# Two weight units of a query projection in Strassen's seven products, and another timetable for early weight sums

## The chip, the cores and the metric

One core of a Trainium2 chip runs the kernel once; the other cores have no part in it. The metric is the device time of that execution in microseconds. TensorE (PE) does the matrix products into eight PSUM banks, VectorE (DVE), ScalarE (ACT) and GpSimd (POOL) work on tiles in SBUF, and DMA queues fed by SyncE (SP) and POOL bring the weights from HBM.

## The reference, cut to what matters

One decoder layer for 256 tokens of width 2048, in float32: a projection for two kinds of attention, the attentions, an output projection, a gated feed-forward block of width 5632, and a gated embedding branch, with RMS norms between.

```python
a = rmsnorm(h, attn_norm)
proj = a @ w_in            # q of 8 latent heads | latent c_kv | shared rope key | q, k, v of 8 block heads
kv = rmsnorm(c_kv) @ w_ukv # keys and values of the latent heads
h += concat(mla_attention(...), moba_attention(...)) @ w_o
f = rmsnorm(h)
h += (silu(f @ w_gate) * (f @ w_up)) @ w_down
g = sigmoid(rmsnorm(h) @ w_ple_gate)
h += g * (p @ w_ple_proj)
return rmsnorm(h)
```

The weights hold nearly all of the data and of the work: each of their 128x512 blocks meets two tiles of 128 tokens.

## The kernel before, in words

**Products.** Both sides of a product are split into a high part in TensorE's rounded float32 type and a low part, the rest. `three` (L392 to L399) makes each product of three matmuls: high by high, low by high (activation's low part, L398), high by low (weight's low part, L399). The weight's high part is a ScalarE copy (`split_hi`, L352), its low part a VectorE subtraction (`split_lo`, L363).

**Units and groups.** A group is one projection of up to 1024 columns; `group` cuts it into units of two 128-row tiles of the weight, mostly a 256x1024 piece of 1 MB. In order the groups are: ga (latent, rope key, part of v), q0 (first 1024 query columns), u0 (keys and values of the first four latent heads; called the key group here, to keep it apart from the up group u0), q1, u1, qk0, qk1, v, wo0, wo1, then gate and up groups g0, u0, g1, d1, u1, and so on to gu5, with pieces of the down projection (d) between, dl, and the last groups. Each plain unit is 24 matmuls of 512 columns (2 row tiles, 2 halves of columns, 2 token tiles, 3 matmuls).

**Strassen units.** In the gate and up groups, and in two units of dl1, a unit's 2x2 block product is made in seven block products instead of eight: 21 matmuls. They come in four turns (`seven`, L439 on), wait for sums of activation blocks (four of them, made by `act_transpose` or `sums_of`) and of weight blocks (L362, L365, L366, made by VectorE in place in the raw buffer after the load). Behind a group's last Strassen unit the products meet in a tile U (L464 to L468), and the group's last unit is added to it (L427).

**Early sums.** For twelve Strassen units of g1 to u4 (the last of a gate group, the last two of an up group) the weight sums are made long before. `early_sums` is a generator, begun at q0's first unit: it loads the unit's 1 MB through POOL's queue into the tile "more_sums" (L375), waits until TensorE has been given 38,400 more columns, does three VectorE operations (L381 to L383), stores the result to HBM (L385) and goes on to the next. The late load of such a unit then brings sums instead of weights, into two raw buffers (L224 to L226).

**Order.** Everything is issued by one loop over units and turns (from L1294); each engine works through its own instructions in that order. In each turn the loop first collects the splits that may be made (`jobs`), issues their high parts, runs `step()`, which moves every waiting task on by one piece (rotations, transposes, attention heads, early sums; L500 on), issues the low parts and then the turn's products. When a split may be issued is set by `plan` (L243 on): high and low parts lie in a ring of 12 places of 512 columns, a job takes places in turn without wrapping, and it may be issued only in a turn behind the one that last used any of them. Plain units take 4 places. From g0 on the ring is longer. The raw buffers are three, from g0 on five.

```python
jb.first = at
jb.wait = max(last.get(x, -1) for x in range(at, at + places))
...
while nxt < len(jobs) and jobs[nxt].unit in raw and jobs[nxt].wait < j and jobs[nxt].unit <= i + (3 if i > 1 else 1) and \
        (jobs[nxt].unit <= i + 2 or i >= wide and units[jobs[nxt].unit].asked < i) and \
        not (u.sevens_end and 0 <= n < 3 and jobs[nxt].unit > i + 1):
    todo.append(jobs[nxt])
```

Behind q0, `after_q_mla` rotates q (L568 to L573, twelve VectorE operations) in the first step of the key group and transposes it in the next (L711).

Of the kernel before, what the change touches and what calls it, by code (L numbers as in the profile page):

```python
# [35 lines left out]
def kernel(ctx, tc, x, p, positions, attn_norm, w_in, kv_norm, w_ukv, w_o, ffn_norm,  # L36
# [152 lines left out]
    def group(name, srcs, ks, chunks, lhs, evac, pool=None, singles=0, per=2, sums=None, sevens=(), adding=(),  # L189
              order=None, swap=False, bank0=0, deep=False, into=None, early=()):  # L190

        pairs = [ks[i:i + 1] for i in range(singles)] + [ks[i:i + per] for i in range(singles, len(ks), per)]
        st = {"banks": None, "begun": set()}
        for i, pr in enumerate(pairs):
            u = Unit()
            u.name, u.srcs, u.ks, u.chunks, u.lhs, u.st = name, srcs, pr, chunks, lhs, st
            u.first, u.last, u.evac, u.pool = i == 0, i == len(pairs) - 1, evac, pool
            u.order = order or [(c, t) for c in range(len(chunks)) for t in range(NT)]
            u.idx, u.store, u.again, u.into = i, None, None, into
# [168 lines left out]
    def early_sums():  # L368

        for u in units:  # L370
            if not u.early:
                continue
            f = big.tile([128, 4, 512], F32, name="wsums", tag="more_sums")
# [4 lines left out]
            while columns[0] < since + 38400:  # L378
                yield 1
# [61 lines left out]
    def seven(u, turn):  # L441
# [18 lines left out]
        if turn == 3 and u.sevens_end:  # L460
            U = S["U"] = big.tile([128, NT, 1024], F32, name="U", tag="vb")
# [14 lines left out]
    def sums_of(parts, k0, pairs, at, tag="vb"):  # L476

        for n, kk in enumerate(pairs):
# [6 lines left out]
            hi, lo = (aT[i][:, at + 2 * n:at + 2 * n + 2] for i in range(2))  # L485
# [5 lines left out]
            split_psum(hi, lo, some)  # L491
            yield 1

    def sum_at(pairs, at):
        def f(k, j):
            o = at + 2 * pairs.index(k) + j // 2
            return tuple(aT[i][:, o, j % 2 * 128:j % 2 * 128 + 128] for i in range(2))
        return f

# [243 lines left out]
    def after_kv(half):  # L743
        def g():
# [4 lines left out]
            yield 1  # L749
            for i in range(4):  # L750
# [74 lines left out]
    oM_alloc()  # L825
# [37 lines left out]
    group("q0", [(wi, 0, 1024)], K16, C2, a_l, q0_evac)  # L863
# [175 lines left out]

    def mixed(name, order=((0, 0), (1, 0), (0, 1), (1, 1))):  # L1040
# [7 lines left out]
                    early=sevens[-2 if name[0] == "u" else -1:] if name[-1] in "1234" else (), order=list(order) if sevens else None,  # L1048
# [40 lines left out]
    LAST_SUMS = (36, 38)  # L1089
    for hc in range(2):  # L1090
        pairs = LAST[hc].split()
        group(f"dl{hc}", [(wd, hc * 1024, hc * 1024 + 1024)], [2 * int(x.strip("S")) + i for x in pairs for i in range(2)],
              C2, ff_l, add_evac(hc * 1024, ssp, norm_half(8 * hc, G_PLE, ssp if hc else None, "rp", 1 if hc else 6)),
              sevens=tuple(i for i, x in enumerate(pairs) if x[0] == "S"), sums=sum_at(LAST_SUMS, 8),
              order=[(0, 0), (1, 0), (0, 1), (1, 1)] if hc else None, deep=True, into=hc * 1024, swap=not hc)
# [198 lines left out]
    for i, u in enumerate(units):  # L1294
        asking[0] = i
        if i < wide:
            load(i + 3)
        if u.name == "q0" and u.idx == 0:
            add(early_sums())
# [8 lines left out]
        if u.name == "dl0" and u.idx == 0:  # L1308
            add(sums_of(ffT[4], 32, LAST_SUMS, 8), 5)
# [6 lines left out]
        for n in range(max(1, len(u.turns))):  # L1316
# [16 lines left out]
            if n % 2 == 0:  # L1333
# [48 lines left out]
```

## Time and profile before

| | |
|---|---|
| median of 3 runs | 1189.46 us (1189.06 to 1189.85) |
| the profiled execution | 1189.34 us |
| its span | 1187.6 us |
| PE, DVE, ACT, POOL busy | 99%, 79%, 60%, 5% |
| splits on DVE, L363, into the ring | 301, 436.5 us |
| splits on ACT, L352, into the ring | 303, 370.4 us |
| HBM read, written | 250.41 MB, 25.17 MB |

The span is the time between the first and the last instruction on the chip. A row of a timeline gives start and duration in us, engine, line, operation, the tile written and those read, with shapes, and in brackets how long the engine had been idle before it and what released it. The table of waits gives the total in us, how often and the longest. A matmul's row lasts longer than it holds TensorE, since matmuls are pipelined; the distance between starts tells the pace.

### The profile page before, as it was taken

The numbers are of one execution on the slowest core, as the hardware profiler recorded it, in microseconds if no ns is written. First come the engines' busy times: TensorE is split into PE (matmuls) and PEld (weight loads), VectorE is DVE, ScalarE is ACT, GpSimd is POOL, SyncE is SP. The second block draws the span as 40 slices with busy tenths as digits, with TensorE's granted clock in tenths as the row PEclk, the third lists the DMA queues.
The fourth block names the chain that finished last, engine by engine and source line by source line (L and its number), as shares of the span: only waits on it lengthen the run. The fifth ranks groups of instructions, "written<-read, shape, count | busy, mean of one in ns | idle before, by whom it ended". The sixth has DMA issues, their size and how long they took to land.

```text
span 1187.6 us, 14600 instructions
## 1 busy us (share of the span) xinstructions
PE 1175.0 (99%) x5486; PEld 982.7 (83%) x5486; DVE 938.5 (79%) x1109; ACT 708.4 (60%) x904; POOL 54.6 (5%) x76
## 2 busy tenths in 40 slices
PE   9999999999999999999999999999999999999996
PEld 7888888899888888888888888888888888888886
DVE  6656656766666678998999898989998999897474
ACT  6735745456555754566657575767575756465453
POOL 5200000000000000000000000000000000000000
PEclk9999999999999999999999999999999999999999
DMA  9775876667784776396978797778878795836631
GB/s 309 244 264 180 293 267 230 227 216 270 258 321 165 283 247 240 107 333 165 336 206 296 214 330 223 261 222 321 237 262 243 266 270 207 339 139 219 209 107 71
DMA packets 86647, 284.92 MB, mean 240 GB/s; under 512 B 5612, under 2 KB 10016, under 8 KB 82224
## 3 DMA queue, kind: packets, MB, share of 16 engines
q1 hardware_dynamic: 77664, 239.36, 56.9%
q0 software_dynamic: 8624, 44.10, 13.7%
q8 instruction: 43, 0.70, 0.2%
q10 hardware_dynamic: 288, 0.52, 0.1%
q14 instruction: 28, 0.23, 0.1%
HBM read 250.41 MB, written 25.17 MB: 232 GB/s over the span
## 4 chain that ended last, share of the span: by engine, by line
PE 90%; DVE 6%; ACT 2%; issue 1%; DMA 1%; ACTq 0%; POOL 0%; DVEq 0%; POOLq 0%
PE bank L399 29%; PE bank L397 28%; PE bank L398 28%; DVE ringl L363 2%; PE bank L138 1%; ACT ringh L352 1%; PE bank L1028 1%; DMA raw<-in_w_o 1%; DVE most L363 1%; PE bank L590 0%; DVE morel L363 0%; PE bank L619 0%; PE bank L593 0%; PE bank L711 0%; ACT att L603 0%
## 5 line engine op out<-in xcount | busy, mean ns | idle before, releaser
L352 ACT CAST ringh<-raw 128x1024 fp32r<-128x1024 f32 (+4 forms) x303 | 370.4, 1258 | 272.2 <-PE bank L398 123.6
L363 DVE TENSOR_TENSOR ringl<-raw,ringh 128x1024 fp32r<-128x1024 f32 (+4 forms) x301 | 436.5, 1473 | 108.2 <-ACT ringh L352 103.7
L397 PE MATMUL bank<-ringh,aT 128*128 128x512 f32 (+3 forms) x721 | 278.5, 386 | 0.0
L399 PE MATMUL bank<-ringl,aT 128*128 128x512 f32 (+3 forms) x721 | 273.6, 380 | 0.1
L398 PE MATMUL bank<-ringh,aT 128*128 128x512 f32 (+3 forms) x721 | 273.4, 379 | 0.0
L399 PEld LDWEIGHTS bank<-ringl,aT 128*128 128x128 f32 x721 | 135.5, 188 | 25.5 <-DVE ringl L363 0.7
L397 PEld LDWEIGHTS bank<-ringh,aT 128*128 128x128 f32 x721 | 135.8, 188 | 23.9 <-ACT aT L124 0.3
L398 PEld LDWEIGHTS bank<-ringh,aT 128*128 128x128 f32 x721 | 135.7, 188 | 23.7
L363 DVE TENSOR_TENSOR morel<-raw,moreh 128x1024 fp32r<-128x1024 f32 (+2 forms) x68 | 87.4, 1305 | 5.1 <-ACT moreh L352 4.5
L352 ACT CAST moreh<-raw 128x1024 fp32r<-128x1024 f32 (+2 forms) x70 | 77.6, 1143 | 21.1 <-DVE raw L362 11.4
L397 PE MATMUL bank<-ringh,ffTh 128*128 128x512 f32 x212 | 82.6, 389 | 0.0
L398 PE MATMUL bank<-ringh,ffTl 128*128 128x512 f32 x212 | 82.5, 389 | 0.0
L399 PE MATMUL bank<-ringl,ffTh 128*128 128x512 f32 x212 | 82.5, 389 | 0.0
L352 ACT CAST most<-raw 128x1024 fp32r<-128x1024 f32 (+2 forms) x58 | 57.7, 1021 | 37.2 <-DVE raw L362 16.4
L363 DVE TENSOR_TENSOR most<-raw,most 128x1024 fp32r<-128x1024 f32 (+2 forms) x58 | 67.6, 1182 | 1.3 <-ACT most L352 1.0
L362 DVE TENSOR_TENSOR raw<-raw 128x1024 f32<-128x1024 f32 x50 | 61.2, 1225 | 1.7
L398 PEld LDWEIGHTS bank<-ringh,ffTl 128*128 128x128 f32 x212 | 39.8, 188 | 8.3
L399 PEld LDWEIGHTS bank<-ringl,ffTh 128*128 128x128 f32 x212 | 39.8, 188 | 8.2
L397 PEld LDWEIGHTS bank<-ringh,ffTh 128*128 128x128 f32 x212 | 39.8, 188 | 8.2
L397 PE MATMUL bank<-moreh,aT 128*128 128x512 f32 x92 | 36.0, 391 | 0.0
L366 DVE TENSOR_TENSOR raw<-raw 128x512 f32<-128x512 f32 x50 | 34.6, 692 | 1.7
L399 PE MATMUL bank<-morel,aT 128*128 128x512 f32 x92 | 35.8, 389 | 0.0
(361 smaller groups left out, 1929.5 us busy)
## 6 DMA issues: line engine op xcount, KB each, us to landing
raw<-in_w_down SPq DMA_DIRECT2D x44, 1024.0 KB, 7.2
raw<-in_w_gate SPq DMA_DIRECT2D x36, 1024.0 KB, 7.2
raw<-in_w_up SPq DMA_DIRECT2D x32, 1024.0 KB, 7.8
raw<-in_w_in SPq DMA_DIRECT2D x40, 512.0 KB, 4.8
raw<-in_w_o SPq DMA_DIRECT2D x16, 1024.0 KB, 7.2
raw<-in_w_ple_gate SPq DMA_DIRECT2D x16, 1024.0 KB, 5.1
raw<-in_w_in SPq DMA_DIRECT2D x8, 1024.0 KB, 4.9
wsums<-in_w_up POOLq DMA_DIRECT2D x8, 1024.0 KB, 7.8
```

Of the source, the lines that this page charges most:

```text
L138: nc.tensor.transpose(b[:, (2 * i + t) * 128:(2 * i + t + 1) * 128], part[:, t, i * 128:(i + 1) * 128], ident)
L352: nc.scalar.copy(h[:, :, c0:c1], r[:, :, c0:c1])
L362: tt(f[:, 0:2], f[:, 1:2].to_broadcast([128, 2, 512]), f[:, 0:4:3], op=ALU.subtract)
L363: tt(l[:, :, c0:c1], r[:, :, c0:c1], h[:, :, c0:c1].bitcast(F32), op=ALU.subtract)
L366: tt(f[:, 2], f[:, 2], f[:, 3], op=ALU.subtract)
L397: nc.tensor.matmul(b, xh, h, start=start, stop=False)
L398: nc.tensor.matmul(b, xl, h, start=False, stop=False)
L399: nc.tensor.matmul(b, xh, l, start=False, stop=stop)
L1028: nc.tensor.transpose(b[:, (2 * i + t) * 128:(2 * i + t + 1) * 128], st[:, t, (k + i) * 128:(k + i + 1) * 128], ident)
```

## The change

Units 5 and 6 of q0 (counted from 0) become Strassen units. Their activation sums are made by `sums_of` from aT in the steps of q0's units 3 and 4 into a tile of their own on the tag "f2h"; U lies on the tag "f0h", and the tile oM, which had these tags from the start, is now made when the first heads begin. q0's plain units now come as two jobs of 2 places each; a Strassen unit takes 2, 1, 2 and 2. In q0's Strassen units `step()` runs only in the first turn, and only if there are free banks.

The early sums begin sooner and in two tiles: one generator from ga's unit 5 for two units in the tile "f0l", another from ga's unit 8 for the others in "more_sums"; both take from one list. The wait is 34,816 columns instead of 38,400, and no sum is made while "crowded" holds: q0 from unit 3 on, v from unit 1 on, wo0 before unit 4. Which units have early sums changes too: g1 has two instead of one, u4 one instead of two; there are twelve as before.

```diff
-    def early_sums():
-
-        for u in units:
-            if not u.early:
-                continue
-            f = big.tile([128, 4, 512], F32, name="wsums", tag="more_sums")
+    todo_early = []
+
+    def early_sums(tag, enough=99):
+
+        made = 0
+        while todo_early and made < enough:
+            u = todo_early.pop(0)
+            made += 1
+            f = big.tile([128, 4, 512], F32, name="wsums", tag=tag)
...
-            while columns[0] < since + 38400:
+            while columns[0] < since + 34816 or S["crowded"]:
                 yield 1
...
-            U = S["U"] = big.tile([128, NT, 1024], F32, name="U", tag="vb")
+            U = S["U"] = big.tile([128, NT, 1024], F32, name="U", tag=u.home)
...
+    def sums_tile(pairs):
+        def f(k):
+            if "four" not in S:
+                S["four"] = big.tile([128, 2, 2, 4, 128], F32R, name="four", tag="f2h")
+            return tuple(S["four"][:, i, pairs.index(k)] for i in range(2))
+        return f
...
+            if half == 0:
+                oM_alloc()
...
-    group("q0", [(wi, 0, 1024)], K16, C2, a_l, q0_evac)
+    SA = sums_tile((10, 12))
+    group("q0", [(wi, 0, 1024)], chunks=C2, lhs=a_l, evac=q0_evac, sums=sum_at(SA), home="f0h",
+          **by_pairs("0 1 2 3 4 S5 S6 7"))
...
+    EARLY = dict(g1=2, u1=2, g2=1, u2=2, g3=1, u3=2, g4=1, u4=1)
...
-                    early=sevens[-2 if name[0] == "u" else -1:] if name[-1] in "1234" else (), order=list(order) if sevens else None,
+                    early=sevens[-EARLY.get(name, 0):] if name in EARLY else (), order=list(order) if sevens else None,
...
+        S["crowded"] = (u.name == "q0" and u.idx > 2 or u.name == "v" and u.idx > 0 or
+                        u.name == "wo0" and u.idx < 4)
+        if u.name == "ga" and u.idx == 5:
+            todo_early.extend(x for x in units if x.early)
+            add(early_sums("f0l", 2))
+        if u.name == "ga" and u.idx == 8:
+            add(early_sums("more_sums"))
         if u.name == "q0" and u.idx == 0:
-            add(early_sums())
+            add(sums_of(aT, 0, (10, 12), SA, "xh"), 3)
...
-            if n % 2 == 0:
+            if n % 2 == 0 and (i >= wide or not u.strassen or n == 0 and B["rot"]):
                 step()
```

The rest of the change gives `sums_of` a function for where its results go, and writes the two dl groups through the new helper `by_pairs`, with the same units and places as before.

More of the change, by code (lines that the diff above doesn't have):

```diff
@@ L189, in group @@
     def group(name, srcs, ks, chunks, lhs, evac, pool=None, singles=0, per=2, sums=None, sevens=(), adding=(),
-              order=None, swap=False, bank0=0, deep=False, into=None, early=()):
+              order=None, swap=False, bank0=0, deep=False, into=None, home="vb", early=()):
         pairs = [ks[i:i + 1] for i in range(singles)] + [ks[i:i + per] for i in range(singles, len(ks), per)]
@@ L198, in group @@
             u.order = order or [(c, t) for c in range(len(chunks)) for t in range(NT)]
-            u.idx, u.store, u.again, u.into = i, None, None, into
+            u.idx, u.store, u.again, u.into, u.home = i, None, None, into, home
             u.strassen, u.sevens_first, u.sevens_end = i in sevens, i in sevens[:1], i in sevens[-1:]
@@ L474, in seven, with sums_of @@
                 add(join())
-    def sums_of(parts, k0, pairs, at, tag="vb"):
-        for n, kk in enumerate(pairs):
+    def sums_of(parts, k0, pairs, dst, tag="vb"):
+        for kk in pairs:
             both = big.tile([128, 2, 2, SEQ], F32, name="both", tag=tag)
@@ L490, in sums_of, with spare_sums, f, sum_at @@
             tt(four[:, 3], a12, four[:, 1], op=ALU.subtract)
-            split_psum(hi, lo, some)
+            split_psum(*dst(kk), four)
             yield 1
[L494 to L497, printed above, removed]
-        return f
+    def spare_sums(pairs, at):
+        def f(k):
+            o = at + 2 * pairs.index(k)
+            return tuple(aT[i][:, o:o + 2].rearrange("q a (b c) -> q (a b) c", b=2) for i in range(2))
+        return f
+    def sums_tile(pairs):
+        def f(k):
+            if "four" not in S:
+                S["four"] = big.tile([128, 2, 2, 4, 128], F32R, name="four", tag="f2h")
+            return tuple(S["four"][:, i, pairs.index(k)] for i in range(2))
+        return f
+    def sum_at(dst):
+        return lambda k, j: tuple(x[:, j] for x in dst(k))
+    def by_pairs(text):
+        pairs = text.split()
+        sevens = tuple(i for i, x in enumerate(pairs) if x[0] == "S")
+        ks = [2 * int(x.strip("S+")) + i for x in pairs for i in range(2)]
+        adding = tuple(i for i, x in enumerate(pairs) if x[-1] == "+")
+        return dict(ks=ks, sevens=sevens, adding=adding, order=[(0, 0), (1, 0), (0, 1), (1, 1)] if sevens else None)
     tasks, posts = [], []
@@ L1088 @@
     LAST = ('16 17 18 19 20 21', '16 S18 S19 17 20 21')
-    LAST_SUMS = (36, 38)
+    SL = spare_sums((36, 38), 8)
     for hc in range(2):
[L1091 to L1095, printed above, removed]
+        group(f"dl{hc}", [(wd, hc * 1024, hc * 1024 + 1024)], chunks=C2, lhs=ff_l,
+              evac=add_evac(hc * 1024, ssp, norm_half(8 * hc, G_PLE, ssp if hc else None, "rp", 1 if hc else 6)),
+              sums=sum_at(SL), deep=True, into=hc * 1024, swap=not hc, **by_pairs(LAST[hc]))
     def p_l(k, t):
@@ L1308 @@
         if u.name == "dl0" and u.idx == 0:
-            add(sums_of(ffT[4], 32, LAST_SUMS, 8), 5)
+            add(sums_of(ffT[4], 32, (36, 38), SL), 5)
         if u.name == "dl0" and u.idx == 2:
```

2 lines of the change are left out of this document (removed).

## The prediction

> **What bounds the kernel now.** I read the page first, then TensorE's waits, then timelines of TensorE and VectorE around each place that the change touches.
>
> ```profile
> span 1187.6 us, 14600 instructions
> PE 1175.0 (99%) x5486; PEld 982.7 (83%) x5486; DVE 938.5 (79%) x1109; ACT 708.4 (60%) x904; POOL 54.6 (5%) x76
> ...
> DVE  6656656766666678998999898989998999897474
> ...
> PE bank L399 <- DVE most L363: 0.9, 1, 0.9
> PE bank L619 <- DVE att L596: 0.3, 1, 0.3
> PE bank L613 <- ACT att L609: 0.3, 1, 0.3
> ```
>
> TensorE is busy for 1175.0 of 1187.6 us, and once it has started its waits are three short ones. So the time is the number of columns that TensorE streams, plus the few places where VectorE's low halves (L363) come late. VectorE has room in the first third (6 tenths) and hardly any from the gate and up groups on (9 tenths). Work taken off TensorE counts in full; work put on VectorE counts only where the split that TensorE wants next stands behind it. The profiled execution took 1189.34 us, 1.74 over its span and 0.12 under the median of 1189.46. All sums below are made against 1189.34.
>
> **Part 1: two Strassen units in q0.** A plain unit is 24 products of 512 columns, a Strassen unit 21. The first unit of the group behind q0 gives the pace and the point at which the second one wants its low half:
>
> ```profile
> 97.16 0.39 PE L397 MATMUL bank<-ringh,ckvT 128*128 128x512 f32 x1
> ...
> 102.61 0.60 PE L711 MATMUL bank<-ident,stage 128*128 128x128 f32 x4
> 102.97 0.48 PE L397 MATMUL bank<-ringh,ckvT 128*128 128x512 f32 x1
> ...
> 103.52 0.40 PE L399 MATMUL bank<-ringl,ckvT 128*128 128x512 f32 x1
> ```
>
> Twenty-four products take 102.61 - 97.16 = 5.45 us, 0.227 each. Six fewer save **1.36 us**, all on the bound engine. The Trainium skill ("TensorE: Matmul & The Clock Gate", section "Wait — 56ns, not 53.3ns?") states N / 2.4 GHz plus about 2.5 ns, which is 216 ns for 512 columns and would make this 1.29 us; the trace's 0.227 is longer, and the measurement decides.
>
> What it adds lies on VectorE. Its row before, and the same operations where the kernel already has them (late groups):
>
> ```profile
> 62.40 2.28 DVE L363 TENSOR_TENSOR ringl<-raw,ringh 128x2048 fp32r<-128x2048 f32 x1
> ...
> 93.64 2.29 DVE L363 TENSOR_TENSOR ringl<-raw,ringh 128x2048 fp32r<-128x2048 f32 x1 [3.15 <-ACT ringh L352]
> 95.85 1.22 DVE L381 TENSOR_TENSOR wsums<-wsums 128x1024 f32<-128x1024 f32 x1
> ...
> 98.44 0.28 DVE L568 TENSOR_TENSOR ra<-stage,tabs 128x128 f32<-128x128 f32 x1
> ...
> 101.55 2.35 DVE L363 TENSOR_TENSOR ringl<-raw,ringh 128x1024 fp32r<-128x1024 f32 x2
> ...
> 912.17 1.22 DVE L362 TENSOR_TENSOR raw<-raw 128x1024 f32<-128x1024 f32 x1
> ...
> 918.92 1.22 DVE L362 TENSOR_TENSOR raw<-raw 128x1024 f32<-128x1024 f32 x1
> ...
> 1015.99 1.28 DVE L427 TENSOR_TENSOR U<-U,bank 128x512 f32<-128x512 f32 x2
> ...
> 1038.42 0.68 DVE L483 TENSOR_TENSOR both<-ffTh,ffTl 128x512 f32<-128x512 f32 x1
> ...
> 1041.46 0.68 DVE L122 TENSOR_TENSOR ffT<-bank,ffT 128x512 fp32r<-128x512 f32 x1
> ...
> 1059.64 0.69 DVE L465 TENSOR_TENSOR U<-U,bank 128x512 f32<-128x512 f32 x1 [0.30 <-PE bank L399]
> ...
> 1062.29 2.35 DVE L363 TENSOR_TENSOR ringl<-raw,ringh 128x1024 fp32r<-128x1024 f32 x2
> ```
>
> A plain split costs 2.2 us (93.64 to 95.85). A Strassen unit without early sums costs 6.75 (912.17 to 918.92), one pair's activation sums 3.04 (1038.42 to 1041.46), forming U 2.65 (1059.64 to 1062.29), an add to U 0.64, an early weight sum 2.59 (95.85 to 98.44), the rotation of q 3.1 (98.44 to 101.55). VectorE is free at 64.7 (62.40 + 2.28), at the third unit's step. From there to the end of q0 it gets one early weight sum (2.6), the plain splits of unit 4, of unit 7 and of the next group's first unit (6.6), two pairs of sums (6.1), two Strassen units (13.5), U (2.65) and four adds (2.55): 34.0 us, ending at 98.7. TensorE ends q0 at 97.16 - 1.36 = 95.80. VectorE, which was a whole unit ahead, is now 2.9 us behind. Inside the group this is just hidden: sixth and seventh unit get their low halves with some tenths to spare.
>
> **Part 2: what stands next in VectorE's queue.** Two things meet at the first unit of the key group (u0 in the code, behind q0).
>
> The first is the ring. It has 12 places. In the old plan each unit has 4, and the key group's second unit takes those of q0's unit 6, so its split is queued in q0's last turn (the row at 93.64). With the change the five plain units end at place 3, the sixth unit gets 4 to 10, the seventh 0 to 6 (its first pair of places doesn't fit at 11), the eighth 7 to 10, the key group's first unit 0 to 3, its second 4 to 7. Place 7 belongs to the eighth unit, so this split can be queued only in the key group's first turn, behind that turn's step.
>
> The second is the step. The tile "f0l" is loaded at ga's unit 5; at ga's unit 8 there are 3 x 11,520 = 34,560 columns, 256 short of 34,816, so its sum runs at q0's unit 0 and its second is due 36,864 columns later, at unit 3, where "crowded" holds it. The tile "more_sums" is loaded at ga's unit 8, summed at q0's unit 2 (36,096 columns), and its next is held as well. At the key group's first unit "crowded" is off, and **both** run, ahead of the rotation of q and of the split.
>
> So VectorE, in order, does 98.7 + 5.2 + 3.1 + 2.2 = 109.2, and with the hand-over TensorE goes on at about 109.2. It wants that low half 103.52 - 97.16 = 6.36 us after q0's end, at 102.16. **Stall: 7.0 us.** If VectorE had no arrears at all, the last add still waits for the last bank: a hand-over (0.30 in the row at 1059.64) and 0.64 after q0's end, so 95.8 + 0.95 + 10.5 = 107.25, a stall of 5.1. With half a microsecond of hand-overs to ScalarE inside the Strassen units it is 7.6. I take 7.0, since the list of work is complete. Nothing behind it gives it back: TensorE is the bound before and after.
>
> Moving the loads of the first sums into ga and the tile "oM" behind the keys I cost at nothing: the first load leaves when POOL has done the rotary angles, as today's does, and U's and the sums' readers end long before head_mla writes "oM". The skipped steps in the two Strassen units cost nothing either; the tasks that could run then are the held sums.
>
> **Part 3: which units have early sums.** g1 gets a second one (its unit 5), u4 loses one (also its unit 5).
>
> ```profile
> 502.99 0.39 PE L398 MATMUL bank<-most,sumsmore_sums 128*128 128x512 f32 x1
> 504.28 0.50 PE L399 MATMUL bank<-most,sumsmore_sums 128*128 128x512 f32 x1 [0.90 <-DVE most L363]
> ...
> 925.66 1.23 DVE L362 TENSOR_TENSOR raw<-raw 128x1024 f32<-128x1024 f32 x1
> ...
> 928.73 1.22 DVE L363 TENSOR_TENSOR most<-raw,most 128x1024 fp32r<-128x1024 f32 x1
> ...
> 930.68 0.39 PE L399 MATMUL bank<-most,sumsmore_sums 128*128 128x512 f32 x1
> ```
>
> The stall at 504.28 is g1's unit 5: 1.29 instead of 0.227, 1.06, with a tenth after it: **1.2 us**, and 2.6 us less on VectorE just ahead of it takes it away. In u4 the third product pair of unit 4 is split at 928.73 + 1.22 = 929.95 and wanted at 930.68, a lead of 0.73. A unit without early sums takes 6.74 on VectorE (918.92 to 925.66) against 21 x 0.227 = 4.77, and loses 1.97. Unit 5 today has early sums and loses nothing; without them its third turn comes 1.97 - 0.73 = 1.24 late, with the tenth **+1.3 us** (0 to 1.5). The stall moves from g1 to u4.
>
> **Part 4: nothing behind the keys.** Three units' columns are now enough for a sum, so the other eight follow at every third unit's worth of columns, the last at v's unit 0; today they run on through v (273.35 below) into wo0.
>
> ```profile
> 266.96 1.48 DVE ringl L363
> ...
> 270.69 0.31 PE L399 MATMUL bank<-ringl,aT 128*128 128x320 f32 x1
> ...
> 271.80 1.48 DVE ringl L363
> 273.35 1.14 DVE wsums L381
> ...
> 275.41 0.31 PE L399 MATMUL bank<-ringl,aT 128*128 128x320 f32 x1
> ...
> 277.36 7.75 DMA raw<-in_w_o
> ...
> 289.27 0.38 PE L620 MATMUL bank<-pTb,vb 128*128 128x128 f32 x2
> 289.96 0.70 PE L619 MATMUL bank<-pTb,vb 128*128 128x256 f32 x2 [0.30 <-DVE att L596]
> ...
> 303.96 0.82 PE L613 MATMUL bank<-ident,att 128*128 128x128 f32 x6
> 305.08 0.84 PE L613 MATMUL bank<-ident,att 128*128 128x128 f32 x3 [0.29 <-ACT att L609]
> 305.84 0.70 PE L619 MATMUL bank<-pTb,vb 128*128 128x256 f32 x2
> ...
> raw<-in_w_o SPq DMA_DIRECT2D x16, 1024.0 KB, 7.2
> ```
>
> In v VectorE loses ground to TensorE; its leads at units 4 and 5 are 270.69 - 268.44 = 2.25 and 275.41 - 273.28 = 2.13. Today's sum (273.35) comes after them; one of 2.6 at unit 0 comes before them: **+0.5** (0 to 0.6). The chain then goes through the load of w_o, which leaves when a raw buffer comes free at 277.36, at the same point either way. It took 7.75 us, the median of its kind is 7.2, and the sums' loads and stores are gone. Behind it TensorE stalls twice: small products take 0.09 each (four from 102.61 to 102.97), but two from 289.27 take 0.69 and nine from 303.96 take 1.88, some 0.5 and 1.1 too long. I take half: **-0.8** (0 to -1.6). The Trainium skill ("Trainium Kernel Development and Optimization", "Key Constraints") says that transfers of all queues interleave on the same 16 DMA engines, by which the POOL queue's traffic does slow this load; how much no row here separates.
>
> **Sum.** -1.36 + 7.0 - 1.2 + 1.3 + 0.5 - 0.8 = +5.4: 1194.8, and with 0.12 for the median **1194.9 us**. With all ends together: -1.36 + 5.1 - 1.2 - 1.6 = +0.9 (1190.3) to -1.36 + 7.6 - 1.2 + 1.5 + 0.6 = +7.1 (1196.6).
>
> **Rivals.**
>
> The split gets ahead (the other side). If the second key unit's split is queued in q0's last turn as today, the weight sums stand behind it and hide under the key group. It decides at one place of the ring: if the eighth unit didn't hold place 7. For it speaks today's order (93.64 ahead of 95.85); against it the places as counted. The 7.0 goes: -1.6, **1187.9 us**, no change that can be told; with u4 free and both w_o stalls gone -4.2, 1185.3, faster. 0.17.
>
> More is late than I count. If VectorE's arrears reach q0's own seventh unit, or its raw buffers come free so late that the keys' loads land late, about 1.5 us come on top: **1196.5** and over. For it: some tenths of slack only. Against: a late group has two such units in a row without a stall, if with a longer ring. 0.07.
>
> The saving isn't had. If the seventh unit waits as long as six products last, the 1.36 is given back within the group; but the same lateness then shortens the later stall, as VectorE's chain is the longer one: 1194.9 again, from other places. 0.04.
>
> **Chances.** The forecast has 0.72. A measurement of this kernel tells 0.2% (2.4 us) from no change. Faster, under 1187.1: a part of the first rival, 0.08. Within 1187.1 to 1191.8: the rest of it, 0.09, and the forecast's low end, 0.08: 0.17. Slower: 0.75. The forecast's own range is 1190.3 to 1196.6; to hold 8 in 10 I take it from 1187.3 to 1197.2, with most of the first rival in it.
>
> **What would show it.** TensorE's waits should show one of 5 to 7.6 us, on L399 of the key group's second unit, ended by VectorE's L363, and VectorE's timeline before it two early sums in a row, twelve rotations, then a 128x2048 split. q0 should be 1.36 us shorter. The 504 wait should be gone and one of about 1.3 us stand one unit (4.8 us) behind the place that is 930.68 today. If the key group's second unit starts its third product without a wait, the forecast is wrong, and the result lies near 1188.

## The result and the profile after

The changed kernel takes 1199.18 us, median of six runs (1197.99 to 1199.93), against 1189.32 of the kernel before in six runs (1189.06 to 1189.85). The ratio is 1.0081, with an interval of 1.0068 to 1.0094: 0.8% slower, by more than the forecast, and above the upper end of its range. The profiled execution took 1197.99 us with a span of 1196.1, 8.5 over the span of before, and is the fastest of the six. Medians are of undisturbed executions: two single ones of later kernels, 1992.82 us with the hold in the keys and 1326.83 us with the filled wait, came at mean granted clocks of 0.56 and 0.84 and are left out.

The page of the kernel after (busy times, then the slices of VectorE and of TensorE's granted clock, the share of full speed that the chip allows it):

```profile
span 1196.1 us, 14660 instructions
PE 1176.1 (98%) x5480; PEld 981.9 (82%) x5480; DVE 957.0 (80%) x1147; ACT 713.1 (60%) x919; POOL 54.4 (5%) x76
...
DVE  5797766857456687998989898989998999897474
...
PEclk9998999999999999999999999999999999999999
```

There are six matmuls fewer (5480 against 5486), and yet PE is busy for 1.1 us more. The slices show why: the fourth, which is 90 to 120 us, has a clock of 8 tenths, and before has 9 or more in all forty. The waits of TensorE (total, how often, longest):

```profile
PE bank L402 <- DVE ringl L363: 8.1, 3, 6.7
...
PE bank L138 <- ACT stage L970: 0.4, 1, 0.4
```

The longest is the one forecast. TensorE's timeline at the key group's second unit (start, duration, line, operation):

```profile
101.88 0.48 PE L400 MATMUL bank<-ringh,ckvT 128*128 128x512 f32 x1
102.20 0.40 PE L401 MATMUL bank<-ringh,ckvT 128*128 128x512 f32 x1
109.28 0.80 PE L402 MATMUL bank<-ringl,ckvT 128*128 128x512 f32 x1 [6.68 <-DVE ringl L363]
109.87 0.63 PE L400 MATMUL bank<-ringh,ckvT 128*128 128x512 f32 x1
110.30 0.63 PE L401 MATMUL bank<-ringh,ckvT 128*128 128x512 f32 x1
...
112.43 0.50 PE L400 MATMUL bank<-ringh,ckvT 128*128 128x512 f32 x1
112.77 0.39 PE L401 MATMUL bank<-ringh,ckvT 128*128 128x512 f32 x1
```

From 102.20 to 109.28 there are 7.08 us where 0.227 belong: the wait costs 6.85. But look at the starts behind it. They stand 0.43 us apart, not 0.227, up to 112.43. Eight steps from 109.28 to 112.77 take 3.49 us where 1.82 belong: another **1.67 us**. The table by stretches (PE, PEld, DVE, ACT, POOL busy, then granted clock, DMA share, GB/s) names the reason:

```profile
104.00:109.00 5.00, 0.00 (x0) 0.00 (x0) 4.76 (x13) 0.08 (x1) 0.80 (x2) 0.68 0.77 315
109.00:113.00 4.00, 3.72 (x10) 2.96 (x10) 2.50 (x3) 0.69 (x1) 0.46 (x1) 0.54 0.70 208
105.82:112.65 6.83, 3.37 (x8) 2.69 (x9) 5.61 (x8) 0.69 (x1) 0.71 (x1) 0.50 0.66 227
```

The clock granted to TensorE falls while it waits and is 0.54 in the stretch in which it starts again. The last row gives the bounds of the half speed: it begins at 105.82, some 3.2 us after the last product ahead of the wait, and ends at 112.65, 3.4 us after TensorE goes on. VectorE's timeline over the wait:

```profile
96.26 2.47 DVE L430 TENSOR_TENSOR U<-U,bank 128x512 f32<-128x512 f32 x4
98.65 1.22 DVE L384 TENSOR_TENSOR wsums<-wsums 128x1024 f32<-128x1024 f32 x1
...
101.24 1.22 DVE L384 TENSOR_TENSOR wsums<-wsums 128x1024 f32<-128x1024 f32 x1
...
106.73 0.29 DVE L592 TENSOR_TENSOR qpT<-qpT,ra 128x128 f32<-128x128 f32 x1
106.94 4.56 DVE L363 TENSOR_TENSOR ringl<-raw,ringh 128x2048 fp32r<-128x2048 f32 x3
```

The four adds end at 98.7, two early sums stand behind them, then the rotation, then the split: the order and the end that Part 2 gave. Three smaller places on TensorE, and what ScalarE does ahead of the second:

```profile
88.00 0.50 PE L402 MATMUL bank<-ringl,four 128*128 128x512 f32 x1
...
400.27 0.95 PE L138 MATMUL bank<-ident,stage 128*128 128x128 f32 x4 [0.45 <-ACT stage L970]
...
943.88 0.50 PE L402 MATMUL bank<-ringl,sumsmore_sums 128*128 128x512 f32 x1 [1.15 <-DVE ringl L363]
```

```profile
396.12 3.70 ACT L352 CAST ringh<-raw 128x2048 fp32r<-128x2048 f32 x2
399.72 1.70 ACT L970 ACTIVATE stage<-h,rs 128x256 f32<-128x256 f32 x4
```

At 400.27, ahead of g0, TensorE waits for a scale on ScalarE that stands behind two casts; the kernel before has no wait there. The account of the spans, in us:

| term | forecast | in the trace |
|---|---|---|
| six products fewer | -1.36 | -1.36 |
| q0's sixth to eighth unit late (0.41 at 88.00, 0.13 at 91.3) | 0 | +0.54 |
| wait in the key group | +7.0 | +6.85 |
| half clock behind it | not thought of | +1.67 |
| g1's unit 5 | -1.2 | -1.17 |
| u4's unit 5 | +1.3 | +1.42 |
| v | +0.5 | +0.40 |
| behind v, heads ahead of wo0 | -0.8 | -0.56 |
| g0's first step | not thought of | +0.89 |

This adds to +8.7. The profiled run was 0.4 earlier at q0's start, which the change doesn't touch; that leaves 8.3 of the 8.5. The median is 1.2 us above the profiled run, where the kernel before has its profiled run at the median; the fourth experiment bears on this.

### The profile page after: what moved, and what is told of

It is laid out like the page before. It is cut to its first block, busy times and chain, and to the rows that moved or that the text cites. A ratio compares the mean times of both kernels' runs of the same rounds, so it can differ in the third digit from the quotient of the medians.

```text
span 1196.1 us, 14660 instructions
## 1 busy us (share of the span) xinstructions
PE 1176.1 (98%) x5480; PEld 981.9 (82%) x5480; DVE 957.0 (80%) x1147; ACT 713.1 (60%) x919; POOL 54.4 (5%) x76
## 4 chain that ended last, share of the span: by engine, by line
PE 89%; DVE 6%; ACT 2%; issue 1%; DMA 1%; SPq 0%; DVEq 0%; ACTq 0%
PE bank L402 28%; PE bank L400 28%; PE bank L401 28%; DVE ringl L363 2%; PE bank L138 1%; ACT ringh L352 1%; PE bank L1050 1%; DMA raw<-in_w_o 1%; PE bank L609 0%; PE bank L730 0%; PE bank L638 0%; PE bank L612 0%; ACT att L622 0%; DVE wsums L384 0%; PE bank L632 0%
## 5 line engine op out<-in xcount | busy, mean ns | idle before, releaser
L352 ACT CAST ringh<-raw 128x1024 fp32r<-128x1024 f32 (+4 forms) x315 | 374.8, 1226 | 266.2 <-PE bank L401 116.7
L363 DVE TENSOR_TENSOR ringl<-raw,ringh 128x1024 fp32r<-128x1024 f32 (+4 forms) x313 | 441.1, 1433 | 94.6 <-ACT ringh L352 90.1
L400 PE MATMUL bank<-ringh,aT 128*128 128x512 f32 (+3 forms) x711 | 274.5, 386 | 0.0
L402 PE MATMUL bank<-ringl,aT 128*128 128x512 f32 (+3 forms) x711 | 270.0, 380 | 0.3 <-DVE ringl L363 0.2
L401 PE MATMUL bank<-ringh,aT 128*128 128x512 f32 (+3 forms) x711 | 269.3, 379 | 0.0
L400 PEld LDWEIGHTS bank<-ringh,aT 128*128 128x128 f32 x711 | 133.8, 188 | 23.4 <-ACT aT L124 0.3
L401 PEld LDWEIGHTS bank<-ringh,aT 128*128 128x128 f32 x711 | 133.7, 188 | 23.3
L363 DVE TENSOR_TENSOR morel<-raw,moreh 128x1024 fp32r<-128x1024 f32 (+2 forms) x68 | 87.5, 1306 | 10.3 <-ACT moreh L352 9.8
L363 DVE TENSOR_TENSOR most<-raw,most 128x1024 fp32r<-128x1024 f32 (+2 forms) x58 | 67.5, 1183 | 2.6 <-ACT most L352 2.4
L362 DVE TENSOR_TENSOR raw<-raw 128x1024 f32<-128x1024 f32 x52 | 63.7, 1225 | 1.7
```

The source lines that it names most:

```text
L352: nc.scalar.copy(h[:, :, c0:c1], r[:, :, c0:c1])
L362: tt(f[:, 0:2], f[:, 1:2].to_broadcast([128, 2, 512]), f[:, 0:4:3], op=ALU.subtract)
L363: tt(l[:, :, c0:c1], r[:, :, c0:c1], h[:, :, c0:c1].bitcast(F32), op=ALU.subtract)
L400: nc.tensor.matmul(b, xh, h, start=start, stop=False)
L401: nc.tensor.matmul(b, xl, h, start=False, stop=False)
L402: nc.tensor.matmul(b, xh, l, start=False, stop=stop)
```

## The experiments

My theory was the forecast's queue: VectorE's arrears from the Strassen units, two early sums and the rotation stand ahead of one split, and the half clock follows from the wait. The rivals: the new timetable of the early sums alone costs the time; the Strassen units alone do; or the half clock is only where the profiler happened to look.

**Split first.** In the key group's first turn the splits are issued before the step.

```diff
+            if u.name == "u0" and u.idx == 0 and i < wide:
+                for jb in todo:
+                    split(jb)
+                todo = []
             if n % 2 == 0 and (i >= wide or not u.strassen or n == 0 and B["rot"]):
```

> One part moved: in the key group's first turn the splits are issued ahead of the step, everything else as in the changed kernel. Queue theory (the 6.7 us wait is order on VectorE: two early sums and the rotation stand ahead of the second unit's split): that split is done some 1.2 us before it is wanted, the wait and the half-speed stretch behind it go, -6.9 and -1.7 to -3.4: 1189 to 1191 us, and VectorE does exactly as much as before. Work rival (two Strassen units, two sums of activations and two weight sums are simply too much for VectorE there): the wait only moves to q1's first units, and 1195 or more stays. Load rival (the second unit's weights or its ring place come late): no change, 1199.

Measured: 1200.97 us, ratio 1.0095 (1.0082 to 1.0108). The forecast of the queue theory fell. The key group's wait shrank to 1.67, as it said, but the profiled run (span 1200.1) has the time elsewhere. TensorE's waits, and VectorE behind the key group:

```profile
PE bank L402 <- DVE ringl L363: 7.7, 5, 4.5
...
PE bank L755 <- DVE qpT L592: 0.7, 1, 0.7
```

```profile
117.98 1.15 DVE L363 TENSOR_TENSOR ringl<-raw,ringh 128x1024 fp32r<-128x1024 f32 x1
125.21 1.23 DVE L384 TENSOR_TENSOR wsums<-wsums 128x1024 f32<-128x1024 f32 x1 [6.08 <-DMA wsums<-in_w_gate]
```

The total on L363 is 7.7 against 8.1: hardly less. The sums, now later, sent their stores and the next load later (POOL issued it at 116.65); the next sum was due by its columns, stood at the head of VectorE's queue, and VectorE stood idle for 6.08 us for its load, with q1's splits behind it. TensorE waited 4.6 there, and its clock halved there too (ten steps from 129.08 to 133.51, 2.2 us lost). The expectation's work rival had named this place and a time like this, but VectorE stood idle ahead of it, so it was not the amount of work. So an order that saves one split doesn't help if the sums stay: they have to go to where nothing wants VectorE.

**Hold in the keys.** No early sum is made in the key group either.

```diff
-        S["crowded"] = (u.name == "q0" and u.idx > 2 or u.name == "v" and u.idx > 0 or
+        S["crowded"] = (u.name == "q0" and u.idx > 2 or u.name == "u0" and i < wide or u.name == "v" and u.idx > 0 or
```

> The hold of early sums is extended over the key group's two units; the order of step and split stays. Queue theory: 5.2 us leave the queue ahead of the split, the rotation (3.1) and 2.9 of arrears stay, so a wait of 1.6 to 1.9 us is left, too short for a half-speed stretch: 1191.5 to 1193.5 us; the two sums then run at q1's first step and may cost up to 0.7 there, and the last sum falls into wo0 instead of v, which takes v's 0.5 away. Work rival: the wait moves to q1 in full, 1197 or more. Load rival: 1199.

Measured: 1192.20 us, ratio 1.0024 (1.0015 to 1.0033), in the range forecast. TensorE's waits and the two stretches:

```profile
PE bank L402 <- DVE ringl L363: 3.0, 3, 1.5
...
PE bank L400 <- ACT stage L879: 1.3, 1, 1.3
```

```profile
104.00:109.00 5.00, 4.01 (x18) 3.31 (x19) 4.97 (x5) 2.40 (x5) 0.00 (x0) 1.00 0.55 169
109.00:113.00 4.00, 4.00 (x21) 3.31 (x20) 3.90 (x6) 3.33 (x5) 0.89 (x2) 1.00 0.96 372
```

One condition, and 7.0 of the 9.9 us are gone: 5.2 of the wait (1.68 is left) and all of the half clock. With that the work rival falls: the wait did not move to q1 in full, where 1.3 us stand at its end. A wait of 1.7 us does not cost the clock. No early sum falls into v here, and none of the waits of v and of the heads behind it is there, although a sum's load is issued in v (at 258.50).

**Plain q0.** q0 has no Strassen unit, the new timetable stays.

```diff
-          **by_pairs("0 1 2 3 4 S5 S6 7"))
+          **by_pairs("0 1 2 3 4 5 6 7"))
...
-        if u.name == "q0" and u.idx == 0:
-            add(sums_of(aT, 0, (10, 12), SA, "xh"), 3)
```

> q0's eight units are plain again (no Strassen units, no sums of activations); the early sums keep the changed timetable, so both still stand in the key group's first step. Queue theory: what hurts is the ring shift that Strassen units bring together with the sums; with four places a unit the split is issued one turn earlier and the sums hide: no wait in q0 or the key group, +1.36 for the 6 products, about 1189.5 to 1190.5 us; the stall at g0's second unit (ring position) goes too. If the two sums alone were too much for that place, a wait of over 3 us would stay on L402 of the key group or q1: 1194 or more.

Measured: 1189.66 us, ratio 1.0000 (0.9992 to 1.0009). The new timetable alone costs nothing, as the theory said: it has the 1.3 in u4 and 0.4 in v, and loses those of 504 and 290. Two sums stand at 96.0 and 98.6, at the key group's start, and TensorE doesn't wait for them, since VectorE is ahead there. The wait at g0 is not there either.

**Fill the wait.** Sixty transposes of 128 columns, whose result nobody reads, stand ahead of the key group's second unit, so that TensorE is not idle in the wait.

```diff
+            if u.name == "u0" and u.idx == 1 and i < wide:
+                b = obank()
+                for _ in range(60):
+                    nc.tensor.transpose(b[:, 0:128], ident, ident)
```

> The wait is kept and filled: 60 transposes of 128 columns (0.109 us each, 6.5 us) that nobody reads stand ahead of the key group's second unit on TensorE. Clock theory: the granted clock halves because TensorE idles; with the fill it stays at 1.0, the stretch of 0.43 us a product behind the wait is gone: 1.7 to 3.4 us less than the changed kernel, 1196 to 1197.5 us, and the runs lie within 0.8 us of one another as those of the kernel before. Rival (the slow products have another cause, such as VectorE and TensorE reading the same memory): no gain or some tenths slower, 1199 to 1200, runs spread over 2 us as now.

Measured: 1196.25 us, ratio 1.0057 (1.0044 to 1.0070), 2.9 below the changed kernel. The stretches, and the product that had waited:

```profile
104.00:109.00 5.00, 5.00 (x46) 4.80 (x44) 4.76 (x13) 0.17 (x1) 0.55 (x1) 1.00 0.77 316
109.00:113.00 4.00, 3.86 (x17) 3.02 (x17) 2.59 (x3) 1.38 (x2) 0.71 (x1) 1.00 0.63 193
```

```profile
109.37 0.50 PE L402 MATMUL bank<-ringl,ckvT 128*128 128x512 f32 x1
109.71 0.39 PE L400 MATMUL bank<-ringh,ckvT 128*128 128x512 f32 x1
```

The split comes no sooner (109.37 against 109.28), the clock stays at 1.00, and the next starts are 0.23 apart. So the half clock is a term of its own, worth 2.9 us in the median. The two profiled spans differ by 1.7 (1196.1 and 1194.4), as the 1.67 of the trace has it. That the other five runs of the changed kernel lost more to it, and that this is the 1.2 by which its median lies above its profile, fits both numbers, but only one of these six runs left a trace.

**Old timetable.** The Strassen units with the early sums timed as before: one generator from q0's first unit, 38,400 columns, no hold. Which units have early sums stays as in the changed kernel.

```diff
-            while columns[0] < since + 34816 or S["crowded"]:
+            while columns[0] < since + 38400:
...
-        if u.name == "ga" and u.idx == 5:
+        if u.name == "q0" and u.idx == 0:
             todo_early.extend(x for x in units if x.early)
-            add(early_sums("f0l", 2))
-        if u.name == "ga" and u.idx == 8:
             add(early_sums("more_sums"))
```

> The changed kernel with its two Strassen units but with the early sums on the timetable of before: one generator from q0's first unit, one tile, 38,400 columns between a load and its sum, no hold in q0's second half. Theory that the held sums make the wait: one sum (2.6 us) falls into the seventh or eighth unit of q0 and one into the key group's first unit, so two places wait some 2 us each, none as long as 6.7, TensorE's clock does not halve, and the 0.9 us at g0 stays: about 1193.5 (1192 to 1195). Rival, that the Strassen units' own arrears on VectorE make the wait and the hold is a help: the key group's wait is as long as with the hold or longer and the sum in q0 adds its own: 1199 or more.

Measured: 1197.53 us, ratio 1.0067 (1.0054 to 1.0080), between the two forecasts. TensorE and VectorE in the key group:

```profile
103.40 0.40 PE L401 MATMUL bank<-ringh,ckvT 128*128 128x512 f32 x1
107.90 0.79 PE L402 MATMUL bank<-ringl,ckvT 128*128 128x512 f32 x1 [4.11 <-DVE ringl L363]
108.49 0.63 PE L400 MATMUL bank<-ringh,ckvT 128*128 128x512 f32 x1
```

```profile
97.46 2.48 DVE L430 TENSOR_TENSOR U<-U,bank 128x512 f32<-128x512 f32 x4
99.85 1.22 DVE L384 TENSOR_TENSOR wsums<-wsums 128x1024 f32<-128x1024 f32 x1
```

One sum in q0 (0.9 of waits there), one in the key group: the wait is 4.28, less than in the changed kernel by one sum of 2.6, and the clock halves here as well (six steps to 110.62, 1.4 us lost). I had counted too few arrears for this run (some 2 us at each of two places, no half clock). So the rival that the Strassen units alone cost the time holds for most of it: they make the kernel slower by 7.9 us even on the old timetable, on which one sum still meets their arrears. The new one adds some 1.7 us, and the two intervals overlap.

**Hold and ring.** The hold as above, and the ring's count put back at wo1, where two Strassen units had moved it by four places.

```diff
+            if u.name == "wo1" and u.first:
+                at = 8
```

> As the run with the hold extended over the key group (1192.2, span 1191.0), and besides the ring's count set to place 8 at the first unit of wo1, which is where it stands there in the kernel before. Ring theory: the 0.9 us that TensorE waits near 394 to 400 us for ScalarE's scale (L970) comes from the ring of split tiles. Two Strassen units use fewer places than two plain ones, so everything behind q0 stands four places lower, and the first split of g0 waits for the place that wo1's unit 6 reads last, where before it waited for the one that unit 5 reads last; its two casts then stand ahead of the scale on ScalarE. With the count put back the wait goes: about 1191.3. Rival: the wait comes from anything else that the two Strassen units shift (all work of ScalarE lies about 1 us earlier against the loads): it stays, about 1192.2.

Measured: 1192.62 us, ratio 1.0024 (1.0014 to 1.0034), no better than without. The wait at g0 is gone, but the table of waits has a new one at wo0's end (lines are two higher here):

```profile
PE bank L404 <- DVE ringl L365: 2.8, 3, 1.5
...
PE bank L402 <- DVE h L919: 1.6, 1, 1.6
```

Two splits, released together by the moved place, stand on VectorE ahead of the additions that empty wo0's accumulators. The theory names the place rightly; its forecast of the time fell.

**Spread.** A plain unit between the two Strassen units and two behind, the activation sums a step sooner, the hold from q0's second unit to the key group's end, and the early sums per group as before.

```diff
-          **by_pairs("0 1 2 3 4 S5 S6 7"))
+          **by_pairs("0 1 2 S5 3 S6 4 7"))
...
-    EARLY = dict(g1=2, u1=2, g2=1, u2=2, g3=1, u3=2, g4=1, u4=1)
+    EARLY = dict(g1=1, u1=2, g2=1, u2=2, g3=1, u3=2, g4=1, u4=2)
...
-        S["crowded"] = (u.name == "q0" and u.idx > 2 or u.name == "v" and u.idx > 0 or
+        S["crowded"] = (u.name == "q0" and u.idx > 0 or u.name == "u0" and i < wide or u.name == "v" and u.idx > 0 or
...
-            add(sums_of(aT, 0, (10, 12), SA, "xh"), 3)
+            add(sums_of(aT, 0, (10, 12), SA, "xh"), 2)
```

> The two Strassen units of q0 are put at the third and fifth place from behind (order of pairs 0 1 2 S5 3 S6 4 7), so that a plain unit stands between them and two plain ones behind the first four evacuations; the sums of aT are begun one unit sooner, the hold reaches from q0's second unit to the end of the key group, and the numbers of early sums in each group are those of before. Theory (VectorE's arrears, not the Strassen work as such): the four additions, the recombination and the splits are spread over five units with slack, no wait above 0.5 us is left in q0 or in the key group and the clock stays full, the 1.36 us of saved products stay saved, and no early sum stands in v: the wait near 504 of the kernel before (1.2 us) comes back, u4's 1.4 goes, the 0.9 at g0 stays as the ring stands at another place than before: about 1188.5 (1187 to 1190). Rival, that any Strassen unit in q0 costs VectorE more than the stage can hide: waits of 2 us or more at q0's end or in the key group, 1191 or more.

> As the run with the Strassen units spread, and the ring's count set to place 8 at wo1's first unit. Ring theory: the 0.9 us at g0 goes as well, 0.9 below the spread run beside it: about 1187.5. Rival: no difference between the two.

Measured: 1199.85 us (1.0084; 1.0070 to 1.0099), and with the ring's count at wo1 1199.80 (1.0085; 1.0071 to 1.0099). Both forecasts of the time fell. From q0's fifth unit to the end of the key group no wait over 0.1 us is left, as the theory said. The time is lost 240 us later. TensorE's waits and VectorE's timeline of the first of the two:

```profile
PE bank L400 <- DVE h L917: 6.3, 1, 6.3
...
PE bank L400 <- ACT stage L879: 1.3, 1, 1.3
```

```profile
342.39 1.23 DVE L384 TENSOR_TENSOR wsums<-wsums 128x1024 f32<-128x1024 f32 x1 [7.50 <-DMA wsums<-in_w_up]
...
347.19 2.47 DVE L917 TENSOR_TENSOR h<-h,bank 128x512 f32<-128x512 f32 x4
```

It is the shape of the first experiment again: the longer hold pushed the twelfth sum behind the hold of v and wo0; VectorE waits 7.50 us for its load, and the additions that empty wo0's accumulators stand behind it. TensorE waits 6.5 us and then runs at half clock to 353.25 (twelve steps, 2.5 us lost; my expectations for the next runs counted eleven of them). With the ring's count at wo1 the wait at g0 is gone, but this one is 2.0 longer.

**The twelfth sum.** Four runs on that: the sums sooner (28,672 columns in place of 34,816), eleven sums in place of twelve, and two with the sums sooner that also hold over q1's end and begin the activation sums one step earlier, one of them with the ring moved on at wo1's fifth unit.

```diff
-            while columns[0] < since + 34816 or S["crowded"]:
+            while columns[0] < since + 28672 or S["crowded"]:
```

```diff
-    EARLY = dict(g1=1, u1=2, g2=1, u2=2, g3=1, u3=2, g4=1, u4=2)
+    EARLY = dict(g1=1, u1=2, g2=1, u2=2, g3=1, u3=2, g4=1, u4=1)
```

```diff
-        S["crowded"] = (u.name == "q0" and u.idx > 0 or u.name == "u0" and i < wide or u.name == "v" and u.idx > 0 or
+        S["crowded"] = (u.name == "q0" and u.idx > 0 or u.name == "u0" and i < wide or u.name == "q1" and u.idx > 3 or u.name == "v" and u.idx > 0 or
...
-            add(sums_of(aT, 0, (10, 12), SA, "xh"), 2)
+            add(sums_of(aT, 0, (10, 12), SA, "xh"), 1)
```

```diff
+            if u.name == "wo1" and u.idx == 4:
+                at = 8
```

> The run with the Strassen units spread (1199.85; profiled at 1200.34 with a span of 1198.5) had no wait left in q0's end or in the key group, but its twelfth early sum stood at 342.39 on VectorE, idle 7.50 us for its load, ahead of the additions that empty wo0's accumulators; TensorE waited 6.5 us for these and then ran at half speed to 353.3 (eleven steps with 2.18 us lost). Here the columns between a load and its sum are 28,672 and not 34,816 (12.7 us of products and not 15.4), so that one more sum lies ahead of the hold in v and wo0. Late-sum theory: the wait at 348 and the half clock go, about 9 us: 1191 (1190 to 1192.5). Rival, that the wait at 348 comes from the shift of the whole schedule and not from the sum: it stays, 1199 or more.

> The spread run with eleven early sums and not twelve (one in u4's group), all else as there. Late-sum theory: with no twelfth sum the wait at 348 and the half clock go, 9 us, and u4's fifth unit waits 1.3 to 1.4 us again as in the changed kernel: about 1192.3 (1191.5 to 1193.5). Rival, a shift of the schedule: the wait at 348 stays, 1200 or more.

> As the run with the sums sooner, and two small waits of the spread run aimed at: the sums of aT are begun one step earlier (the 0.5 and 0.5 us at 71 to 72, where TensorE waits for their split), and the hold reaches over q1's last four units, where an early sum at 131.07 stood ahead of the softmax steps and ScalarE emptied q1's accumulators late (1.5 us at 139.58). Theory that both waits come from the place of these sums in VectorE's queue: 2 to 2.5 us below the run beside it, about 1188.7 (1187.5 to 1190). Rival: a sum held back in q1 comes as late in the chain of sums as the twelfth did and gives the wait before wo1 back: 1196 or more.

> As the run before it in this list, and the ring's count moved on by four places at wo1's fifth unit, not at its first as in the run with hold and ring, where the 0.9 us at g0 went but 1.7 us came at 343, two splits standing ahead of wo0's last additions. Ring theory: g0's first split waits for the place that wo1's sixth unit reads last, as in the kernel before, the 0.9 us near 394 goes, and no new wait comes at wo0's end: 0.9 below the run beside it, about 1187.8. Rival: the wait moves into wo1, no difference.

Measured: 1198.12 (1.0070; 1.0057 to 1.0084), 1191.50 (1.0017; 1.0008 to 1.0026), 1200.54 (1.0094; 1.0081 to 1.0108) and 1200.98 (1.0095; 1.0082 to 1.0109). Only the run with eleven sums settles it: without the twelfth the wait and the half clock are gone, 8.35 us, and u4's 1.3 is back:

```profile
PE bank L400 <- ACT stage L879: 1.3, 1, 1.3
PE bank L402 <- DVE ringl L363: 1.2, 1, 1.2
PE bank L402 <- DVE most L363: 0.9, 1, 0.9
PE bank L138 <- ACT stage L970: 0.5, 1, 0.5
```

In the other three the eleventh sum still stood behind the hold of v and wo0, the twelfth came as late as before (340.15 to 343.1), and the wait of 6.4 to 6.9 stayed; there my forecasts missed by the whole of it. The first of them lost the wait of 1.3 at q1's end that the spread run has at 139.58, since its sum there stood at 126.0 and not at 131.1. The hold over q1 took that wait away too, but the activation sums begun a step earlier were no help: TensorE waits 1.9 to 2.2 for them at 75. With the ring moved at wo1's fifth unit the wait at g0 went, and three of 0.29 came in wo1.

**A sum in v.** As the run with the sums sooner, with the hold of v from its fourth unit on; and the same with the ring moved on at wo1's third unit.

```diff
-        S["crowded"] = (u.name == "q0" and u.idx > 0 or u.name == "u0" and i < wide or u.name == "v" and u.idx > 0 or
+        S["crowded"] = (u.name == "q0" and u.idx > 0 or u.name == "u0" and i < wide or u.name == "v" and u.idx > 2 or
```

```diff
+            if u.name == "wo1" and u.idx == 2:
+                at = 0
```

> As the spread run with the sums sooner (1198.12), and the hold in v begins with its fourth unit and not with its second, so that the eleventh early sum, whose load was issued at 248.06, falls into v and the twelfth behind the hold at some 316, as the eleventh did there. Late-sum theory: the 6.74 at 345.77, the 0.34 behind it and 2.5 us of half clock go, some 0.4 come in v as in the changed kernel: 1189.0 (1188.3 to 1190), that is level with the kernel before or 0.4 under it. What is left then is 0.5 at 71, 0.9 at g0 and 1.1 at 512, against 1.2 near 305 and 1.1 near 504 before, and 1.36 saved. Rival: the sum in v costs more than 0.4 there, since v's splits have a lead of 3 us: 1190 to 1192.

> As the run beside it, and the ring's count is moved on by four places at wo1's third unit, so that g0's first split waits for the place that wo1's sixth unit reads last, as in the kernel before. Ring theory: the 0.9 us at g0 goes, and as the move lies further from g0 than in the run where three waits of 0.29 came instead at 374 to 387: about 1188.1, 0.9 below the run beside it. Rival: small waits of wo1's transposes take its place, 1189.0.

Measured: 1190.44 us (1.0008; 0.9999 to 1.0017), in the rival's range and not in the theory's, and 1189.24 us (0.9999; 0.9990 to 1.0008). With a sum in v the waits near 290 and 305, which the runs without one had lost, are back (0.5 and 0.75). The twelfth sum now stands at 318.9 and 317.5, and nothing waits for it. The ring's move is worth 1.2 us between the two (forecast 0.9), and the wait at g0 is not there in the second; this time nothing came in its place. TensorE's waits of the second (lines two higher, without the start's 2.0):

```profile
PE bank L404 <- DVE most L365: 0.9, 1, 0.9
PE bank L634 <- ACT att L630: 0.3, 1, 0.3
PE bank L403 <- DVE four L122: 0.2, 1, 0.2
PE bank L404 <- DVE ringl L365: 0.2, 1, 0.2
...
```

These are before's waits near 504 and 305 (that near 290 is cut off here), and two new places: 0.69 at 70 to 71, where TensorE waits for the activation sums, and 0.39 at 269.83 in v. So 1.08 of the saved 1.36 are spent again, and the kernel with two Strassen units in q0 ends level with the kernel before. No version that I tried is measurably faster than it.

## Why the prediction was wrong

**The queue behind q0 was right.** The adds end at 98.7 as worked out, the split at 109.3 (forecast 109.2), and the wait is 6.85 (forecast 7.0). The experiments show all its parts: the two sums are 5.2 of it (1.68 is left with the hold), and the arrears of the Strassen units are needed too (none of it with a plain q0). The two halves are not alike: the new timetable without the Strassen units costs nothing, while the Strassen units on the old timetable still cost 7.9 us, through one early sum and the half clock behind a wait of 4.28. Only spread out, with the sums held and moved, are they level with the kernel before.

**The step that failed is the sum itself.** It read "-1.36 + 7.0 - 1.2 + 1.3 + 0.5 - 0.8", and Part 2 closed with "Nothing behind it gives it back". Nothing did, but the wait had a second price: TensorE starts again at half speed. That term, put at nothing, is 1.67 us in the profiled run and 2.9 in the median, shown by filling the wait, and with it in the sum the forecast would have been 1197.8. The 1.4 that is left to 1199.18 is about what the next two places cost, 0.89 and 0.54. The Trainium skill ("TensorE: Matmul & The Clock Gate", section "What's actually happening") says that the clock drops to half after at least one idle window of about 3.4 us and comes back after at least one such busy window, that the windows run freely, and that the number of slow matmuls at a kernel's start varies from run to run. The traces agree on the drop as far as they reach: no half clock behind waits of 1.3 to 2.2 us, half clock behind all of 4.3 to 8.5, and no wait in between. The half speed began 2.2 to 5.0 us after the last product, in two runs (2.2 and 2.3) sooner than one such window. The stretches of half speed, wait and restart together, are 3.41 us (old timetable), 6.83 (the changed kernel and three others) or 10.24 long (three runs), so one, two or three times 3.41. Behind the restart the slow steps took 3.5 us in the changed kernel's profile, and from 2.7 to 6.1 over all runs; the six runs of the changed kernel spread over 1.94 us where the kernel before spreads over 0.79. The prediction cites this page of the Trainium skill for a pace and passes over what it says of a wait of 7 us.

**The ring was followed only as far as the key group.** Part 2 counted the places up to the wait. But every place behind q0 stands four lower than before, up to g0, where the first split waits for one unit more and its casts stand ahead of a scale: +0.89. The pair of runs with and without the ring's move shows it (1.2 us, and the wait gone). Moving it at another place made waits elsewhere, so the price belongs to the whole order and not to one place.

**"Just hidden" was 0.54.** The tenths to spare in q0's sixth to eighth unit were not there; which of the hand-overs that were left out took them, no run separates. Losses of this size were not in the range, whose upper end had room for 0.6 us alone.

**The -0.8 behind v had the wrong cause.** Part 4 let w_o's second load leave "at the same point either way" and took the gain from a faster load, rid of the sums' traffic. The load is no faster: 7.75 us before, 7.74 in the changed kernel, where the last sum's store had landed 14 us before it was issued, and 7.3 with the hold in the keys. What moves is its start, counted back from v's last product: 9.4 us before, 10.0 in the changed kernel, 12.0 with the hold in the keys, which has no sum in v. The load waits for a raw buffer, the buffer for VectorE's split, and v's splits stand behind the sum. Here is ScalarE's cast of that load, ahead of the next steps of the attention heads, in the changed kernel and then with the hold in the keys:

```profile
292.63 1.91 ACT L352 CAST ringh<-raw 128x2048 fp32r<-128x2048 f32 x1 [0.59 <-DMA raw<-in_w_o]
```

```profile
286.52 1.90 ACT L352 CAST ringh<-raw 128x2048 fp32r<-128x2048 f32 x1 [1.47 <-PE bank L401]
```

The first waits for the load, the second for TensorE. In the six runs without an early sum in v the heads' waits are gone altogether, although in some of these a sum's load is issued there; with one sum in v they are there in part or in whole. So it is the sum's time on VectorE. The change got -0.56.

**The two in the gate groups were right:** -1.17 and +1.42, as forecast to a tenth.

**The rivals.** "The split gets ahead" priced the whole wait at 7.0 once the split stood first. The first experiment put it first and the time went up: the sums took their time from the next splits. That rival's number, 1187.9, was wrong as well; it needs the sums gone from that stretch, not only another order. "The saving isn't had" came in part: 0.54 of the 1.36 was given back within q0, and did not shorten the later wait by as much (6.85 against 7.0). "More is late" was nearest, but for other reasons than it gave.

## What to carry to other kernels

Price a wait of the bounding engine twice: its length, and what the engine does when it starts again. Here a wait of 6.85 us cost some 9.8 in the median, while waits up to 2.2 cost only themselves. Work that fits "somewhere" on an engine with room has to be placed against the order of its queue: on an in-order engine a step that waits for a load holds everything behind it, and a hold that clears one stretch pushes the last piece into another. When a plan hands out places in turn, a change of one early unit moves all later ones; follow it to the next point at which the count is set anew.

## What the runs showed of the hardware

The start of the kernel aside, TensorE's clock halved in every wait of 4.3 us or more and in none of 2.2 or less, for 3.41, 6.83 or 10.24 us in all; the loss behind it was 1.4 us (old timetable, 4.3 of a wait) to 2.9 (sums sooner, 6.7 of a wait) in profiled runs, and 2.9 in the median of the changed kernel, whose profile shows 1.67. Filling the wait with transposes that nobody reads kept the clock at 1.00 and made the kernel 2.9 us faster without any of its own work coming sooner. And what a late sum costs is set by its load: in the spread run the 1 MB were issued at 332.4, VectorE came to wait for them at 334.9 and went on at 342.39, and that turned a sum with room around it into a wait of 6.5 us on TensorE.
